# Wider spreads of the key roots, angle steps placed around the first product, and the convolution given out one quad sooner

## The chip, the cores and the metric

The kernel runs on one core of one Trainium2 chip. The metric is the device time of one execution in microseconds (us), the median of several runs. The engines are TensorE (PE, matrix products), VectorE (DVE), ScalarE (ACT), GpSimd (POOL) and SyncE (SP, which only issues DMAs here).

## The reference

One layer of a gated parallel decoder block, for 2048 tokens of width 1024, all in float32:

```python
h = rms_norm(x, norm_w) * (1 + scale) + shift            # shift, scale, gate from silu(c) @ w_ada + b_ada
a, b, g_conv, q, k, v, g_attn, m_conv, m_attn = split(h @ w_in)
u = depthwise_causal_conv(a * sigmoid(b), conv_w, conv_b)     # 31 taps
y_conv = (silu(layer_norm(u)) * silu(g_conv)) @ w_conv_out
q, k = rope(rms_norm(q)), rope(rms_norm(k))              # per head of 128
o = softmax-weighted sum over three groups of dilated causal windows, 4 heads each
y_attn = (o * silu(g_attn)) @ w_attn_out
out = x + gate * ((sigmoid(m_conv) * y_conv + sigmoid(m_attn) * y_attn) @ w_out)
```

Windows and dilations of the groups are (128, 1), (512, 4) and (2048, 16). The angle of rope is the token's position times a frequency; its cosine and sine are tables of 64 frequencies by 2048 tokens. The root of the mean square of a head enters q and k as a factor for each token.

## The kernel before

**Products.** A float32 product is made of three products of split operands: each operand is a high part (an activation on ScalarE) and the rest (a subtraction on DVE or POOL). The projection h @ w_in is worked in two halves of 1024 tokens. Within a half it goes by *quads*: two columns of 128 channels by two blocks of 512 tokens, made with seven products in place of eight (Strassen's scheme, `PRODUCTS` in line 164), from the quarters A11, A12, A22 and sums S1 to S4 of h. The first job of half 0 is plain instead, with sixteen products (`PLAIN`, line 299) for the v columns of two pairs of heads. One product is twelve matmul instructions (lines 305 to 309) and is called a *slot*; the order of slots is written out in advance (lines 1006 to 1029), and PE works through it in program order.

**The agenda.** Everything else is hung on slots. `at_slot(s, f, where)` (line 465) enters a piece of work, and the loop over slots (lines 1442 to 1483) runs, in this order: what is entered as `enter`, `load`, `act`, `pe`, `vec`; the split of the weights three slots ahead (`prepare`); `act2`; the slot's own product with its eviction; `tail`; `store`; the splits of landed quarters; and `run_conv`. Every engine is a queue in this written order (`manual_schedule`), so an instruction that waits holds up all that stands behind it on its engine. `tail` work of PE comes behind the twelve instructions of its slot.

**The start** (lines 1120 to 1191). h is made from x by a root of the mean square of each token and by scale and shift. ScalarE squares (`x_square`), PE sums (`x_sum`), DVE copies the rows of sums (`x_rows`), PE turns them and POOL takes the root (`x_roots`), PE spreads the roots over partitions (`x_spread`), DVE multiplies (`x_scale`); PE makes scale and shift from `w_ada` (`ada_mm`), and `ada_mod` adds the bias; `first_part` makes the high and the low part of a quarter. `angles()` yields the nineteen steps of the tables, DVE work but for the two sines of step 17; nine are issued before the sums, eight behind the roots, two behind the scaling. `tables_turn` (POOL) orders the tables for the dilated groups and `tables_keep` stores them (SP); they are read again at slot 19. The second block of tokens and the second part of the modulation follow in the slots 0 to 7 (`start_0` to `start_5`).

**Queries and keys** (`rotate`, lines 574 to 692). For a quad of two heads, ScalarE squares, PE sums over the head's channels into one bank (`sums`), ScalarE evicts the sums (`rows`), PE turns them (`turned`), DVE adds the epsilon (`more`), POOL raises to the power -1/2 (`roots`). For a query that is all; the root is applied later. For a key, PE spreads the roots over the channels by products with the identity (`spread`, line 629), one call for each half of the tokens, both into a bank of the tag "t", of which there is one; DVE multiplies (`key_scale`, line 635). The names are `rsk` (the bank), `stk` (mean squares and roots), `pssk` and `pssq` (sums).

**Gates and convolution.** The rest of a half are 22 quads: eight `ab_quad` make a * sigmoid(b), the other fourteen make gates. `gate_jobs` (line 995) orders them: `FIRST_GATES` gates, then each ab quad followed by `BETWEEN` gates. An ab quad that ends enters the 50 operations of its convolution (`conv_parts`, nearly all on DVE), and `run_conv` gives out 3.1 of them a slot (`CONV_RATE`). What is left is given out at once in slot 4 of the second half (`rope_again`). The attention of the half's last heads runs beside the first gates. In the last two quads of half 0 the quarters of the second half are loaded (line 1469), and two slots later they are split.

## Time and profile before

| | us |
|---|---|
| median of 3 runs (lowest, highest) | 2428.83 (2426.19, 2432.19) |
| profiled execution, its own time | 2426.46 |
| its span, from the first to the last instruction | 2424.7 |
| PE busy | 2321.6 (96%) |
| DVE, ACT, POOL busy | 1764.5, 1071.8, 1090.0 |

A row of the timeline gives the start, the duration, the engine, the line, the operation, what it writes and reads, its shape, how many instructions were merged, and in brackets the idle time of the engine before it with what ended it. A row of groups gives count, busy time, mean length in ns and idle time before. The granted clock is 1.00 when PE had its full clock. Names carry no buffer numbers: `paq`, `pak`, `pav` are banks of query, key and value quads, `spare_hi` and `spare_lo` the scratch in which a quad's result stands, `ce`, `cq`, `us`, `ca` the tiles of the convolution.

### The profile page before, as it was taken

The page shows a single profiled execution, that of the slowest core. Times are in us where ns is not written, and L with a number is a line of the kernel's source. Part 1 is how long each engine was busy: PE and PEld are TensorE (multiplying, and loading weights), DVE is VectorE, ACT ScalarE, POOL GpSimd, SP SyncE. Part 2 cuts the span into 40 slices and gives each one's busy share as a digit, 9 for nine tenths or more (in the row PEclk, how much of TensorE's full clock was granted, in tenths as well). Part 3 has the DMA queues.
Part 4 walks back from the last instruction along what each step waited for, and adds up shares of the span by engine and source line. Part 5 has one row for each costly group of instructions (what it writes and reads, how often), then busy time and mean ns, then how long its engine had stood idle before and what let it go on. Part 6 is the DMA issues. An engine that isn't in the chain of part 4 may idle for free.

```text
span 2424.7 us, 35722 instructions
## 1 busy us (share of the span) xinstructions
PE 2321.6 (96%) x12054; PEld 1884.0 (78%) x12054; DVE 1764.5 (73%) x2926; ACT 1071.8 (44%) x2159; POOL 1090.0 (45%) x844
## 2 busy tenths in 40 slices
PE   5998899999999999989999999999999999999999
PEld 3776678878778888767788887887888877888887
DVE  6877685553899999936666447469999988787644
ACT  3664445445554444634445444653444444332221
POOL 3455554445446688835433433445566640000221
PEclk8999999999999999989999999999999999999999
DMA  8366666567544446643565665856445469865553
GB/s 300 116 190 208 212 192 191 177 201 240 181 159 159 152 161 202 197 148 105 172 181 176 192 183 155 266 165 190 142 131 155 140 212 331 302 236 187 178 157 109
DMA packets 304111, 451.61 MB, mean 186 GB/s; under 512 B 29236, under 2 KB 132788, under 8 KB 303928
## 3 DMA queue, kind: packets, MB, share of 16 engines
q1 hardware_dynamic: 289656, 423.62, 55.1%
q10 hardware_dynamic: 14272, 25.72, 2.9%
q8 instruction: 95, 1.56, 0.3%
q14 instruction: 88, 0.72, 0.1%
HBM read 284.98 MB, written 164.24 MB: 185 GB/s over the span
## 4 chain that ended last, share of the span: by engine, by line
PE 72%; DVE 9%; DMA 3%; issue 2%; POOL 1%; ACT 1%; SPq 0%; DVEq 0%; ACTq 0%; POOLq 0%
PE yc L1518 7%; PE paab L309 6%; PE oa L1800 4%; PE pak L309 3%; PE paq L309 3%; PE pag_ma_d L309 3%; PE pcab L309 3%; PE pav L309 3%; PE pag_mc_d L309 3%; PE po L809 3%; PE ya L1518 3%; PE ps L756 3%; PE pag_g_d L309 2%; PE pck L309 2%; PE pcq L309 2%
## 5 line engine op out<-in xcount | busy, mean ns | idle before, releaser
L247 POOL TENSOR_TENSOR slT<-wT,shT 128x512 fp32r<-128x512 f32 x188 | 254.1, 1352 | 314.0 <-ACT shT L246 266.7
L247 POOL TENSOR_TENSOR slB<-wB,shB 128x512 fp32r<-128x512 f32 x142 | 193.4, 1362 | 151.7 <-ACT shB L246 144.4
L246 ACT ACTIVATE shB<-wB 128x512 fp32r<-128x512 f32 x234 | 147.2, 629 | 197.2 <-issue 40.5
L247 POOL TENSOR_TENSOR slT<-wB,shT 128x512 fp32r<-128x512 f32 x98 | 131.0, 1341 | 192.0 <-ACT shT L246 171.2
L246 ACT ACTIVATE shT<-wT 128x512 fp32r<-128x512 f32 x192 | 120.2, 627 | 149.4 <-issue 22.5
L367 DVE SCALAR_TENSOR_TENSOR ce<-ut,chan,ce 128x512 f32<-128x512 f32 x240 | 180.3, 751 | 3.7
L396 DVE SCALAR_TENSOR_TENSOR ce<-us,pair_taps,ce 128x512 f32<-128x512 f32 x240 | 180.7, 753 | 3.1
L768 DVE CUSTOM_DVE_ANT_0 sm<-ps,mask,rqq 128x256 f32<-128x256 f32 (+1 forms) x192 | 78.1, 444 | 120.5 <-PE ps L756 93.3
L380 DVE SCALAR_TENSOR_TENSOR cq<-ut,chan,cq 128x512 f32<-128x512 f32 x208 | 156.2, 751 | 0.0
L241 POOL TENSOR_TENSOR wB<-wB,wB 128x512 f32<-128x512 f32 x80 | 112.5, 1407 | 47.8 <-DVE slB L247 35.8
L246 ACT ACTIVATE shT<-wB 128x512 fp32r<-128x512 f32 x120 | 75.3, 627 | 78.5 <-PE paab L309 25.7
L786 DVE COPY pT<-ptp 128x512 f32<-128x512 f32 (+2 forms) x96 | 58.9, 614 | 55.0 <-PE ptp L784 54.9
L137 POOL TENSOR_SCALAR stf<-stf 128x4 f32<-128x4 f32 x4 | 2.1, 516 | 188.2 <-DVE stf L1556 141.8
L247 DVE TENSOR_TENSOR slB<-wB,shB 128x512 fp32r<-128x512 f32 x92 | 71.4, 776 | 16.8 <-ACT shB L246 14.6
L809 PE MATMUL po<-v,pT 128*128 128x128 f32 x560 | 81.9, 277 | 0.0
L1728 ACT ACTIVATE yh<-yq 128x512 fp32r<-128x512 f32 x48 | 27.3, 623 | 120.6 <-POOL yq L1722 46.4
L809 PEld LDWEIGHTS po<-v,pT 128*128 128x128 f32 x560 | 74.9, 191 | 6.1 <-issue 1.5
L756 PE MATMUL ps<-qk 128*128 128x128 f32 x512 | 75.6, 275 | 0.0
L756 PEld LDWEIGHTS ps<-qk 128*128 128x128 f32 x512 | 66.2, 192 | 0.3 <-issue 0.2
L775 ACT ACTIVATE sm<-sm,osb 128x256 f32<-128x256 f32 (+1 forms) x128 | 58.4, 459 | 8.7 <-DVE osb L768 3.3
L617 POOL TENSOR_TENSOR stk<-stk,mhalf 128x16 f32<-128x16 f32 x12 | 38.4, 3203 | 49.6 <-DVE stk L613 37.9
L815 ACT ACTIVATE osb<-po 128x256 f32<-128x256 f32 x64 | 24.7, 385 | 74.7 <-PE po L809 73.8
(808 smaller groups left out, 7758.2 us busy)
## 6 DMA issues: line engine op xcount, KB each, us to landing
wB<-in_w_in_dram SPq DMA_DIRECT2D x274, 256.0 KB, 4.3
wT<-tT_d SPq DMA_DIRECT2D x152, 256.0 KB, 3.0
tT_d<-wB SPq DMA_DIRECT2D x114, 256.0 KB, 3.5
qk<-qk_d SPq DMA_DIRECT2D x96, 256.0 KB, 4.3
v_d<-vev SPq DMA_DIRECT2D x48, 256.0 KB, 3.3
qk_d<-spare_hi SPq DMA_DIRECT2D x48, 256.0 KB, 3.8
qk_d<-spare_lo SPq DMA_DIRECT2D x48, 256.0 KB, 3.7
v<-v_d SPq DMA_DIRECT2D x96, 128.0 KB, 4.0
```

The costliest lines, as they stand in the source:

```text
L241: nc.gpsimd.tensor_tensor(dst, x0, x1, op=ALU.subtract)
L246: nc.scalar.activation(h, q[name], AF.Copy)
L247: eng.tensor_tensor(l, q[name], h.bitcast(F32), op=ALU.subtract)
L309: nc.tensor.matmul(ps, x, y, start=(first and m == 0), stop=(last and m == 11), skip_group_check=True)
L367: stt(box["e"], e[:, 1 + j : 513 + j], chan[:, cb, 2 * j : 2 * j + 1], box["e"], op0=ALU.mult, op1=ALU.add)
L380: stt(box["o"], o[:, 2 + j : 514 + j], w, psum_o, op0=ALU.mult, op1=ALU.add)
L396: stt(dst, box["both"][:, 1 + j : 513 + j], pair_taps[:, cb, j : j + 1], box["e"], op0=ALU.mult, op1=ALU.subtract if j == 0 else ALU.add)
L756: nc.tensor.matmul(ps[:, c : c + P], box["q"][i], kt, start=True, stop=True)
L768: nc.vector.tensor_tensor_reduce(sm[:, a:z], ps[:, a:z], m[:, 256 - (z - a) :], rq[:, b, u % 2 : u % 2 + 1], 3e38, ALU.add, ALU.min, box[" ...
L809: nc.tensor.matmul(po[:, P * i : P * i + P], box["pT"][:, c : c + P], vt, start=(m == 0), stop=(m == count[i] - 1))
L1518: nc.tensor.matmul(pz, w, xx, start=(m == 0), stop=(m == len(terms) - 1))
L1800: nc.tensor.matmul(ps, y, w, start=(m == 0 and ps.name not in begun), stop=(m == 11 and not more), skip_group_check=True)
```

## The change

- The epsilon is added by ScalarE as the sums are evicted (`rows`, now with a bias), `turned` moves from behind the product of its slot into its middle (a new place `mid`, after six of the twelve instructions), and `more`, now a copy, moves from DVE in the next slot to ScalarE behind the same slot's product.
- For a key, ScalarE widens the roots to 64 columns each (`widen`, two activations of 512 columns), and one `spread` makes eight full products of 128 columns in place of sixteen of 64, in the slot in which the first half was spread before, with a bank for each half ("t" and "u"). `key_scale` stays where it was. The first sums of squares come one slot later, since they use "u" as well.
- In the start, five angle steps stand before the sums, two behind the roots, three behind the scaling, and nine in the slots 1 to 3. The turns of the tables move from POOL to ScalarE, in the slots 4 to 6, and into landing buffers; their stores move to the slots 4 to 7. The second part of the modulation is made one slot sooner, the row of it is evicted before slot 4's product, A12 is made behind slot 4, and the last four scalings move behind slot 5.
- In half 0 two gates stand before the first ab quad in place of three, and three behind the last in place of two.
- The landing buffers of the quarters are six in place of four, and their splits come three slots after the load in place of two.

```diff
@@ -38,7 +38,7 @@
 GROUPS = (1, 2, 0)
 WS, WR, AHEAD = 4, 10, 3
 QKV_LO = (((1, 3, 5), (1, 3, 5), (0, 1, 3, 5, 6)), ((), (), (1, 3, 5)))
-FIRST_GATES, BETWEEN = 3, ((1, 1, 1, 1, 2, 1, 2, 2), (1, 1, 2, 1, 1, 1, 1, 3))
+FIRST_GATES, BETWEEN = (2, 3), ((1, 1, 1, 1, 2, 1, 2, 3), (1, 1, 2, 1, 1, 1, 1, 3))
 CONV_RATE = 3.1
 MANUAL, ORDER_END = (True, True), 6
 LATER_X, LATER_ROOM, LATER_BUSY = 21, 2, 1
@@ -139,6 +139,8 @@
 
     edge = ctx.enter_context(pool("edge", side="right"))
     edge_tile = edge.tile([P, 56], F32, name="edge")
+    eps = edge_tile[:, 55:56]
+    nc.gpsimd.memset(eps, EPS)
     hpool_c = [tc.tile_pool(name=f"hT{i}", bufs=1, side="right", reuse_waits="tile") for i in range(2)]
     hpools = [c.__enter__() for c in hpool_c]
 
@@ -307,6 +309,8 @@
         terms = [t for k in range(4) for t in ((wh[:, k], ah[:, k]), (wh[:, k], al[:, k]), (wl[:, k], ah[:, k]))]
         for m, (x, y) in enumerate(terms):
             nc.tensor.matmul(ps, x, y, start=(first and m == 0), stop=(last and m == 11), skip_group_check=True)
+            if m == 5:
+                run_agenda(slot_now[0], "mid")
 
     def quad(name, got, sink):
 
@@ -600,7 +604,7 @@
 
         def rows():
             r = box["rows"] = rb["p"].tile([P, 2, P], F32, tag="rows", name=f"ssr{n}", bufs=1)
-            nc.scalar.activation(r.rearrange("p c i -> p (c i)"), box["pr"][:, : 2 * P], AF.Copy)
+            nc.scalar.activation(r.rearrange("p c i -> p (c i)"), box["pr"][:, : 2 * P], AF.Identity, bias=eps)
 
         def turned():
             pt = box["pt"] = bank("t", f"prq{n}")
@@ -610,7 +614,7 @@
         def more():
             st = box["st"] = rb["p"].tile([P, 32], F32, tag="st", name=f"st{n}", bufs=2)
             got = box["pt"][:, : 2 * P].rearrange("p (c q m) -> p c q m", c=2, q=4)[..., :2]
-            nc.vector.tensor_scalar(st[:, :16].rearrange("p (c q m) -> p c q m", c=2, q=4), got, EPS, None, op0=ALU.add)
+            nc.scalar.activation(st[:, :16].rearrange("p (c q m) -> p c q m", c=2, q=4), got, AF.Copy)
 
         def roots():
             st = box["st"]
@@ -620,19 +624,22 @@
                 nc.gpsimd.tensor_scalar(rq, st[:, 16:32], ISQ, None, op0=ALU.mult)
                 heads_rq[half, u0] = rq.rearrange("p (b m) -> p b m", m=2)
 
-        def spread(c):
-            def f():
-                rs = box["rs"] = bank("t", f"rs{n}_{c}")
+        def widen():
+            box["wide"] = rp["p"].tile([P, 16, 64], F32, tag="wide", name=f"rw{n}", bufs=1)
+            for c in range(2):
+                sl = slice(8 * c, 8 * c + 8)
+                nc.scalar.activation(box["wide"][:, sl], box["st"][:, 16 + 8 * c : 24 + 8 * c][:, :, None].to_broadcast([P, 8, 64]), AF.Copy)
+
+        def spread():
+            box["rs"] = [bank("tu"[c], f"rs{n}_{c}") for c in range(2)]
+            for c in range(2):
                 for q in range(4):
-                    for m in range(2):
-                        a = 16 + 8 * c + 2 * q + m
-                        nc.tensor.matmul(rs[64 * m : 64 * m + 64, P * q : P * q + P], box["st"][:, a : a + 1].to_broadcast([P, 64]), ident,
-                                         start=True, stop=True, skip_group_check=True)
-            return f
+                    w = box["wide"][:, 8 * c + 2 * q : 8 * c + 2 * q + 2].rearrange("p m r -> p (m r)")
+                    nc.tensor.matmul(box["rs"][c][:, P * q : P * q + P], w, ident, start=True, stop=True)
 
         def key_scale(c, i):
             x = reg[i][:, 512 * c : 512 * c + 512]
-            return lambda: tt(x, x, box["rs"], op=ALU.mult)
+            return lambda: tt(x, x, box["rs"][c], op=ALU.mult)
 
         def store(i):
             def f():
@@ -667,7 +674,7 @@
             count = (2,) * 6
         for s, c, i in sq:
             at_slot(s, square(c, i), "act" if s > e6 else "act2")
-            at_slot(max(s, e6 - 2), sums(c, i), "tail")
+            at_slot(max(s, e6 - 1), sums(c, i), "tail")
         ops = rope()
         assert sum(count) == 12
         for d, k in enumerate(count):
@@ -676,15 +683,16 @@
                 at_slot(start + d, lambda: next(ops)())
         end = start + len(count)
         at_slot(last, rows, "act")
-        at_slot(last, turned, "tail")
-        at_slot(last + 1, more)
+        at_slot(last, turned, "mid")
+        at_slot(last, more, "tail")
         at_slot(last + 1, roots)
         if which == 0:
             for i in range(2):
                 at_slot(end, store(i), "load")
         else:
+            at_slot(last + 2, widen, "act2")
+            at_slot(last + 2, spread, "tail")
             for c in range(2):
-                at_slot(last + 2 + c, spread(c), "tail")
                 for i in range(2):
                     at_slot(last + 3 + c, key_scale(c, i))
             assert last + 3 + 1 >= end - 1
@@ -908,9 +916,12 @@
             nc.tensor.matmul(acc[32 * q : 32 * q + 32, :256], wide[:, k], landed_ada(g, k)[:, q // 2, 256 * (q % 2) : 256 * (q % 2) + 256],
                              start=(k == 0), stop=(k == KC - 1))
 
-    def ada_mod(g, acc, tag):
+    def ada_row(g, acc):
         row = su.tile([P, 512], F32, tag="sq", name=f"row{g}", bufs=5)[:, :256]
         nc.scalar.activation(row, acc[:, :256], AF.Copy)
+        return row
+
+    def ada_mod(g, row, tag):
         pa = bank(tag, f"pt_ada{g}")
         for i in range(2):
             nc.tensor.transpose(pa[:, P * i : P * i + P], row[:, P * i : P * i + P], ident)
@@ -958,17 +969,19 @@
         yield lambda: v.tensor_tensor(a, a, a, op=ALU.mult)
         yield lambda: v.tensor_scalar(a, a, -2.0, 1.0, op0=ALU.mult, op1=ALU.add)
 
-    def tables_turn(g):
-        for src, dst in ((ang, permuted), (sng, nag)):
-            if g == 1:
-                nc.gpsimd.tensor_copy(dst.rearrange("p (t r i) -> p t r i", t=2, r=4), src.rearrange("p (t i r) -> p t r i", t=2, r=4))
-            else:
-                nc.gpsimd.tensor_copy(dst.rearrange("p (r t i) -> p r t i", t=2, r=16), src.rearrange("p (t i r) -> p r t i", t=2, r=16))
-
-    def tables_keep(g):
-        for i, src in enumerate((permuted, nag) if g else (ang, sng)):
-            for half in range(2):
-                nc.sync.dma_start(tab_d[half, g, i], src[64 * half : 64 * half + 64])
+    def table(g, i):
+        return landing[4 - 2 * g + i][:, :1024] if g else (ang, sng)[i]
+
+    def table_turn(g, i):
+        src, dst = table(0, i), table(g, i)
+        if g == 1:
+            nc.scalar.activation(dst.rearrange("p (t r i) -> p t r i", t=2, r=4), src.rearrange("p (t i r) -> p t r i", t=2, r=4), AF.Copy)
+        else:
+            nc.scalar.activation(dst.rearrange("p (r t i) -> p r t i", t=2, r=16), src.rearrange("p (t i r) -> p r t i", t=2, r=16), AF.Copy)
+
+    def table_keep(g, i):
+        for half in range(2):
+            nc.sync.dma_start(tab_d[half, g, i], table(g, i)[64 * half : 64 * half + 64])
 
     turning = angles()
 
@@ -995,7 +1008,7 @@
     def gate_jobs(half):
         todo = [(gate_quad, half, g, cb) for g in ((MC0, mc_d, AF.Tanh), (MA0, ma_d, AF.Tanh), (GC0, g_d, AF.Silu)) for cb in range(0, KC, 2)]
         todo[9:9] = [(ag_quad, half, None, cb) for cb in (0, 2)]
-        got = [todo.pop(0) for _ in range(FIRST_GATES)]
+        got = [todo.pop(0) for _ in range(FIRST_GATES[half])]
         for cb in range(KC):
             got.append((ab_quad, half, None, cb))
             for _ in range(BETWEEN[half][cb]):
@@ -1117,13 +1130,13 @@
         for j in range(2):
             weight(j, name)
 
-    angle_steps(9)
+    angle_steps(5)
     pm = bank("t", "xm0")
     for k in range(KC):
         x_square(k, 0)
         x_sum(k, 0, pm)
     st = x_roots(0, pm, x_rows(0, pm))
-    angle_steps(8)
+    angle_steps(2)
     pr = x_spread(0, st, bank("u", "xr0"))
     acc = bank("o", "ada0")
     for k in range(KC):
@@ -1132,12 +1145,11 @@
     prepare(1)
     for k in range(KC):
         x_scale(k, 0, pr)
-    angle_steps(2)
-    ada_mod(0, acc, "t")
+    angle_steps(3)
+    ada_mod(0, ada_row(0, acc), "t")
     for k in range(4):
         first_part("A11", k, 0)
     prepare(2)
-    tables_turn(1)
 
     box = {}
 
@@ -1171,24 +1183,31 @@
             ada_mm(1, box["acc"], k)
 
     def start_5():
-        ada_mod(1, box["acc"], "t")
+        ada_mod(1, box["row"], "t")
+
+    def start_6():
         for k in range(4, KC):
             first_part("A12", k, 0)
-        for k in range(4, KC):
-            x_scale(k, 1, box["pr"])
 
     at_slot(0, start_0, "tail")
     at_slot(1, start_1, "pe")
     at_slot(1, start_2, "tail")
     at_slot(2, start_3, "tail")
-    at_slot(4, start_4, "tail")
-    at_slot(5, start_5, "tail")
+    at_slot(3, start_4, "tail")
+    at_slot(4, start_5, "tail")
+    at_slot(4, start_6, "tail")
     for k in range(4, KC):
+        at_slot(5, lambda k=k: x_scale(k, 1, box["pr"]), "tail")
         at_slot(6 + (k - 4) // 2, lambda k=k: first_part("A22", k, 1), "tail")
-    at_slot(1, lambda: tables_keep(0), "store")
-    at_slot(1, lambda: tables_keep(1), "store")
-    at_slot(2, lambda: tables_turn(2), "store")
-    at_slot(4, lambda: tables_keep(2), "store")
+    at_slot(4, lambda: box.update(row=ada_row(1, box["acc"])), "act2")
+    at_slot(1, lambda: angle_steps(3))
+    at_slot(2, lambda: angle_steps(4))
+    at_slot(3, lambda: angle_steps(2))
+    for i, (g, s, to) in enumerate(((1, 4, 5), (2, 5, 6), (1, 6, 7), (2, 6, 7))):
+        at_slot(s, lambda g=g, i=i: table_turn(g, i // 2), "act2")
+        at_slot(to, lambda g=g, i=i: table_keep(g, i // 2), "store")
+    for i in range(2):
+        at_slot(4, lambda i=i: table_keep(0, i), "store")
 
     tt = lambda dst, x0, x1, op: nc.vector.tensor_tensor(dst, x0, x1, op=op)
     stt = lambda dst, x0, by, x1, op0, op1: nc.vector.scalar_tensor_tensor(dst, x0, by, x1, op0=op0, op1=op1)
@@ -1466,9 +1485,9 @@
         if i == half_jobs - 1:
             asked += [(PRODUCTS[n][0], k) for k in range(4)]
         for name, k in asked[:2]:
-            raw = gpa["p"].tile([P, 512], F32, tag="ai" if k == 3 else "gt", name=f"landing{name}_{k}", bufs=2 if k == 3 else 4)
+            raw = gpa["p"].tile([P, 512], F32, tag="ai" if k == 3 else "gt", name=f"landing{name}_{k}", bufs=2 if k == 3 else 6)
             nc.sync.dma_start(raw, quarter_src(name, k))
-            held.append((s + 2, lambda name=name, k=k, raw=raw: quarter_split(1, name, k, raw, nc.gpsimd if k == 3 else nc.vector)))
+            held.append((s + 3, lambda name=name, k=k, raw=raw: quarter_split(1, name, k, raw, nc.gpsimd if k == 3 else nc.vector)))
         del asked[:2]
         due += CONV_RATE
         if not conv_todo:
```

## The prediction

> **What bounds the kernel now.** I read the page first, then the busy time by stage, then the waits of TensorE (PE), then the timeline at each of its longer stops.
>
> ```profile
> span 2424.7 us, 35722 instructions
> PE 2321.6 (96%) x12054; PEld 1884.0 (78%) x12054; DVE 1764.5 (73%) x2926; ACT 1071.8 (44%) x2159; POOL 1090.0 (45%) x844
> ```
>
> PE is busy for 96% of the span, so a microsecond is won only where PE stops, where its clock is halved, or where it has less to do. About 103 us of the span are stops. The stages show where (the columns are the stretch and its length, busy time of PE, PEld, DVE, ACT and POOL with their instructions, granted clock, DMA share, GB/s):
>
> ```profile
> 35.00:80.00 45.00, 37.62 (x228) 24.99 (x229) 23.65 (x32) 16.87 (x28) 17.71 (x11) 0.77 0.48 167
> 160.00:400.00 240.00, 218.76 (x1269) 170.96 (x1268) 170.30 (x242) 115.58 (x211) 122.08 (x79) 0.98 0.63 202
> 740.00:985.00 245.00, 245.00 (x1082) 202.89 (x1081) 235.89 (x343) 108.77 (x188) 195.25 (x156) 1.00 0.49 169
> 985.00:1070.00 85.00, 69.37 (x290) 55.45 (x289) 66.14 (x83) 40.53 (x68) 49.05 (x34) 0.90 0.50 160
> ...
> 600.00:620.00 20.00, 20.00 (x114) 17.18 (x113) 11.12 (x41) 12.20 (x37) 6.06 (x8) 1.00 0.51 162
> ...
> 700.00:720.00 20.00, 16.20 (x89) 13.30 (x88) 20.00 (x46) 9.46 (x26) 10.31 (x9) 1.00 0.48 158
> ```
>
> PE stands still for 7.4 us from 35 to 80 (with a mean clock of 0.77), 21.2 us in the key and query quads from 160 to 400, and 15.6 us at the change of halves (985 to 1070). With the wait for the first product, at 35, these are the places that the change touches. From 740 to 985 PE never stops (245 / 1082 = 0.23 us a product, so 2.7 us for a slot of twelve), but DVE is at 96% there: the convolution has it nearly full. The list of PE's waits gives who ended them, their sum, number and longest:
>
> ```profile
> PE rsk L629 <- POOL stk L617: 13.1, 6, 4.2
> ...
> PE rsk L629 <- DVE spare_lo L635: 6.4, 4, 2.1
> ...
> PE pssk L597 <- ACT sqk L584: 4.1, 2, 2.5
> ...
> PE rsk L629 <- DVE spare_hi L635: 3.1, 2, 1.7
> ```
>
> **The change part by part: the start.** Rows of the timeline before (start, duration, engine, line):
>
> ```profile
> 10.57 3.44 PE L880 MATMUL xm<-xsq,ones 128*32 128x128 f32 x40 [0.45 <-ACT xsq L875]
> ...
> 16.32 1.23 DVE L955 SCALAR_TENSOR_TENSOR spare_hi<-spare_hi 128x1024 f32<-128x1024 f32 x1
> 17.46 0.28 DVE L885 COPY xrow<-xm 128x128 f32<-128x128 f32 x1
> ...
> 20.62 2.08 PE L897 MATMUL xr<-ident,xst 128*128 128x128 f32 x8 [2.28 <-POOL xst L892]
> ...
> 26.61 4.86 DVE L902 TENSOR_TENSOR hf<-hf,xr 128x512 f32<-128x512 f32 x8
> ...
> 34.95 0.80 PE L309 MATMUL pC<-A_hi,shB_p 128*128 128x512 f32 x1 [4.28 <-ACT A_hi L937]
> 35.51 0.69 DVE L939 TENSOR_TENSOR A_lo<-hf,A_hi 128x512 fp32r<-128x512 f32 x1
> 36.12 0.55 DVE L938 TENSOR_SCALAR hf<-hf,mod 128x512 f32<-128x512 f32 x1
> ...
> 38.93 4.69 POOL L964 COPY spare_lo<-spare_hi 128x1024 f32<-128x1024 f32 x2
> 41.80 2.37 DVE L939 TENSOR_TENSOR A_lo<-hf,A_hi 128x512 fp32r<-128x512 f32 x1
> ...
> 44.23 0.80 PE L309 MATMUL pC<-A_lo,shB_p 128*128 128x512 f32 x1 [2.97 <-DVE A_lo L939]
> ...
> 45.38 1.51 PE L880 MATMUL xm<-xsq,ones 128*32 128x128 f32 x24
> ...
> 48.69 0.52 PE L309 MATMUL pC<-A_lo,shB_p 128*128 128x512 f32 x1
> ```
>
> The sums of squares end at 14.0 (10.57 + 3.44), but the copy of their rows comes behind nine angle steps and starts at 17.46. With five steps ahead of it it can start at once, 3.4 us sooner, and the spread, 5.2 us later on this row (20.62 + 2.08 - 17.46), ends at about 19.3. Then the eight scalings (4.86) run from 19.3 to 24.2 instead of behind the angles at 26.61; three angle steps (1.23 each) end at 27.9; the modulation and the first part took 34.95 - 33.7 = 1.3 us from DVE's work on the modulation. First product at about 29.3: **-5.6 us**. In the first slot the twelve products took 45.38 - 34.95 = 10.4 us, because the fourth low part waited: 2.37 us for a subtraction that takes 0.69, beside POOL's table copies of 4.69. Those copies go to ScalarE slots later, so a part costs 0.55 + 0.69 and four parts set a slot of about 6.4 us (1.3 + 3 x 1.24 + three products at half speed, since the clock before was not granted in full from 34.95 to 48.69): **-4 us**. The full clock came 4.5 us after the last stop, at 44.23; what is left at half speed in the second slot is worth **-1 us**.
>
> By the Trainium skill ("TensorE: Matmul & The Clock Gate", What's actually happening) one busy window of some 3.4 us opens the clock. By it the second half of the new first slot would already run at full speed, and the sum would be 1 us better. The rows above agree only so far: products with stops between them did not open it in 13.7 us.
>
> ```profile
> 71.24 0.51 PE L309 MATMUL pC<-A_hi,shB_p 128*128 128x512 f32 x1 [1.30 <-ACT A_hi L937]
> ...
> 72.55 0.57 PE L309 MATMUL pC<-A_lo,shB_p 128*128 128x512 f32 x1 [0.81 <-DVE A_lo L939]
> ...
> 78.60 0.63 PE L309 MATMUL pC<-A_lo,shB_p 128*128 128x512 f32 x1
> 79.03 0.63 PE L309 MATMUL pC<-A_hi,slB_p 128*128 128x512 f32 x1
> ```
>
> The second modulation comes one slot sooner, so A12 has a whole slot (some 2.8 us) to be made. The stops of 1.30 and 0.81 us go, and with them the half clock from 72.55 to 79.03 (15 products 0.43 apart against 0.23: 3.2 us). DVE still needs 1.24 us for a part that PE uses in 0.7, so I leave 1 us of wait: **-4.3 us**. What moves into these slots: nine angle steps on DVE in the slots 1 to 3 (at most 9 x 1.23 = 11 us; PE's own work there, three slots of 2.7 with the sums, spread and modulation products between them, is some 15), the sines on ScalarE in slot 2 ahead of A21, four table turns on ScalarE in the slots 4 to 6 ahead of the splits of weights, and the twelve table stores on SP, whose readers come at slot 19. A turn of 1024 columns takes twice what 512 take below, 1.3 to 2.2 us; behind it on ScalarE stand the splits for three slots later, and past that cover PE would wait, so 0 to 4 us lost. Start in all: -14.9, less 1 for this, **-14** (-7 to -18).
>
> **The roots of the keys.** The page's row of a contiguous activation of 512 columns, then one key quad of the timeline, then the two kinds of spread (each product shows as two instructions):
>
> ```profile
> L246 ACT ACTIVATE shB<-wB 128x512 fp32r<-128x512 f32 x234 | 147.2, 629 | 197.2 <-issue 40.5
> ...
> 209.60 1.11 ACT L505 ACTIVATE spare_hi<-paq 128x512 f32<-128x512 f32 x1 [2.02 <-PE paq L309]
> ...
> 216.08 3.31 POOL L617 TENSOR_TENSOR stk<-stk,mhalf 128x16 f32<-128x16 f32 x1 [2.64 <-DVE stk L613]
> ...
> 219.44 0.98 PE L629 MATMUL rsk<-ident,stk 128*64 128x128 f32 x7 [4.15 <-POOL stk L617]
> ```
>
> ```profile
> 55.49 1.05 PE L897 MATMUL xr<-ident,xst 128*128 128x128 f32 x8
> ...
> 56.30 0.48 PE L309 MATMUL pC<-A_hi,shB_p 128*128 128x512 f32 x1
> ...
> 1179.80 1.09 PE L629 MATMUL rsk<-ident,stk 128*64 128x128 f32 x16
> 1180.82 0.66 PE L784 MATMUL ptp<-ident,sm 128*128 128x128 f32 x4
> ```
>
> The mean squares waited on DVE until 216; POOL, free at 213.4, stood 2.64 us for them, and PE then 4.15 for POOL. Moved to ScalarE the copy follows the eviction (209.60 + 1.11) and is done by 210.9, so POOL raises to the power from 213.4 to 216.8, widening (512 columns: 0.63 like the contiguous row, at most the 1.11 of the strided eviction) adds 0.6 before the first half can be spread, and PE waits for about 2 instead of 4.15. So the 13.1 us fall to POOL's own backlog; I take half, **-6.5**. The 9.5 us (6.4 + 3.1) are the second half waiting for the one bank that DVE still read; it has its own bank now: **-9.5**. The first sums of squares come a slot later: of the 4.1 us of waits on ScalarE's squares I take **-3**. Halved clock after the two stops of 4 us is worth **-3** (240 us at 0.98 are 4.8).
>
> PE's own work: the sixteen instructions of eight half-wide products took 1.02 us until the next began (1179.80 to 1180.82), the eight of four full ones 0.81 (55.49 to 56.30). Half-wide pairs already run two at a time, so halving their number saves little; 0.2 for each of 24 spreads, **-5** (0 to -7).
>
> The Trainium skill ("TensorEngine Tiling (Array Packing)", Theoretical Speedup) gives products of at most 64 columns up to twofold speed, as two tiles work side by side. By it four full products take as long as eight half-wide ones, and the sum would be 5 us smaller; the rows agree but for 0.21 us.
>
> Added: 24 widenings of 0.6 us on ScalarE and 24 copies of 16 values (the rows with the bias added are the activation of before). ScalarE is a queue in order: behind a widening that waits for the power stand the eviction of the next product and the splits. No row shows it; the bounds are 0 and the present 13.1, and as ScalarE is at 48% I take 0.4 a quad, **+5**. PE also meets DVE sooner (adds, key scales; the stage has DVE at 71%): **+5** of its gain given back. Transposing the rows inside the product costs nothing while the eviction of the rows precedes it, else up to 1 us a quad. Sum -6.5 - 9.5 - 3 - 3 - 5 + 5 + 5: **-17** (0 to -28).
>
> **Convolution one quad sooner.**
>
> ```profile
> 1015.18 0.80 PE L309 MATMUL pav<-A_hi,shB 128*128 128x512 f32 x1 [5.48 <-ACT spare_hi L446]
> ...
> 1029.94 7.88 DVE L396 SCALAR_TENSOR_TENSOR ce<-us,pair_taps,ce 128x512 f32<-128x512 f32 x10
> ...
> 1042.34 0.77 PE L309 MATMUL pcv<-S_hi,shT 128*128 128x512 f32 x1 [9.06 <-DVE spare_hi L507]
> ```
>
> A block of channels is 50 DVE operations, 3.1 of them are given out in a slot. The last block becomes ready 14 slots before the half ends, so 43 fit and the rest stands ahead of the adds of the second half. Now it has 21 slots: twelve fewer operations in the last 14 slots and none behind them, some 20 of 0.79 us (7.88 / 10), 16 us. That is as much as PE's stops of 15.6, and the half clock that follows them (85 us at 0.90, about half of it with PE at work) is worth 4. I take **-17** of these 19.6. The work goes to the quad before, where DVE has room (11.1 of 20 us from 600 to 620) but attention still runs: once both overlap DVE is full and PE loses up to 3.8 us in 20 (700 to 720). One quad more of it is **+2** (0 to 6). The landing buffers and their splits a slot later hide behind it, since a part is used some twelve slots later, in the next half.
>
> **Sum**: -14 - 17 - 17 + 2 = -46 us against the profiled execution, 2426.46 (a span of 2424.7 and 1.8 around it), so 2380.5. The median of the runs, 2428.83, lies 2.4 above: **2383 us**.
>
> **Rivals.**
> 1. The hole at the change of halves stays: DVE, at 96% from 740 on, only moves its backlog, and PE pays in the attention instead. For it: PE already stops there. Against it: 9 idle us of DVE from 600 to 620. Then -17 + 2 becomes -3: 2395.
> 2. The roots gain nothing: POOL's backlog and ScalarE's blocked queue eat the 17 us: 2400. For it: POOL starts at 213.4 whatever DVE does.
> 3. The start goes better and POOL falls in step (-18, -28, -19, 0): 2429 - 65 = 2364.
> 4. Slower: ScalarE stands at each widening behind POOL's power; the eviction of the next product stands behind it, and PE stops for the bank, with its clock halved afterwards. The other parts bring 14 + 17 - 2 = 29 us, so it decides from 29 / 12 = 2.4 us lost in each of the twelve key quads; with the present longest stop, 4.15, in each it is 50 - 29 = 21 slower: 2450. Against it: the longest stop at a spread now is 4.2, the mean of the six 2.2, and ScalarE is half idle.
>
> **How the numbers follow.** The forecast has 0.6, the rivals 0.14, 0.12, 0.10 and 0.04. The range from 2362 to 2405 holds the first four and leaves out little beyond. A change under 0.3% (7 us) can't be told from none: faster 0.94, same 0.02, slower 0.04.
>
> **What would show it.** The first product near 29 us, no half clock near 73; spread waits under 8 us in all, none on key scales; no PE stop over 3 us between 985 and 1070; slightly more stops on attention's minima from 600 on. It is wrong if ScalarE's widening becomes PE's releaser, if convolution still runs past the half, or if splits behind the table turns stop PE before 90 us.

## The result, and the profile after

The changed kernel takes 2396.46 us (median of 4 runs, 2391.25 to 2400.4) beside 2430.51 of before (4 runs): a ratio of 0.9855, 95% interval 0.9821 to 0.9889. Timed again later beside other runs it took 2394.76 us against 2428.96, 0.9869 (0.9856 to 0.9883). So it is 1.3 to 1.5% faster, 32 to 35 us where 46 were forecast; the time lies in the range forecast, 12 to 14 us above its likeliest value. The execution whose profile follows took 2400.4, the longest of its four.

The page's head, then the same stretches as before (columns as in the prediction: stretch, length, busy PE, PEld, DVE, ACT, POOL, clock, DMA share, GB/s):

```profile
span 2398.6 us, 35365 instructions
...
PE 2319.5 (97%) x11862; PEld 1892.1 (79%) x11862; DVE 1751.2 (73%) x2902; ACT 1093.7 (46%) x2211; POOL 1083.1 (45%) x841
```

```profile
35.00:80.00 45.00, 39.81 (x255) 28.36 (x255) 34.09 (x44) 27.76 (x34) 9.87 (x7) 0.87 0.52 170
160.00:400.00 240.00, 219.37 (x1201) 175.05 (x1201) 167.61 (x237) 117.40 (x221) 119.68 (x78) 0.96 0.61 196
985.00:1070.00 85.00, 79.42 (x354) 65.16 (x353) 48.84 (x58) 46.75 (x78) 52.44 (x36) 0.96 0.59 191
```

The start and the change of halves (985 on) have fewer stops and a better clock. The key and query quads of the first half (160 to 400) are as full of stops as before, and at a lower clock (0.96 against 0.98). The list of PE's waits shows what took the place of the old ones (sum, number, longest):

```profile
PE rsk L638 <- ACT rwk L631: 12.3, 4, 4.9
...
PE pav L311 <- ACT spare_hi L450: 5.6, 1, 5.6
PE pta L838 <- DVE osb L820: 5.5, 3, 3.8
...
PE prqk L612 <- ACT ssrk L607: 4.3, 2, 2.4
```

The 9.5 us on the key scales are gone. The 13.1 us behind POOL's power are now 12.3 behind ScalarE's widening (13.8 in a second execution), and the transposition in the midst of a product brought 4.3 of its own.

Where the time went is seen best by the start of the same product before and after. The table gives, for a profiled execution of each kernel, how much shorter (-) or longer (+) each stretch became: the start of the product that ended the stretch in the new trace less its start before (155.2, 529.8, 965.5, 1085.4 and 1513.0 us), less the same difference at the stretch before; the last column takes the rest from the spans. The second of these products is the first of a gate: the last key quad of the half ends just ahead of it, with its second spread at 524.49 in the profile before. The experiments of the next section stand beside it.

```profile
524.49 1.09 PE L629 MATMUL rsk<-ident,stk 128*64 128x128 f32 x16 [1.74 <-DVE spare_hi L635]
```

| kernel | ratio of times (95%) | start | keys, half 0 | attention, gates | change of halves | keys, half 1 | rest |
|---|---|---|---|---|---|---|---|
| changed | 0.9855 (0.9821-0.9889) | -7.5 | -2.4 | +4.8 | -11.7 | -10.4 | +1.2 |
| changed, timed again | 0.9869 (0.9856-0.9883) | -8.5 | -5.2 | +4.8 | -12.8 | -10.3 | +1.4 |
| start alone | 0.9966 (0.9953-0.9979) | -10.6 | +0.2 | +0.3 | +1.2 | +2.0 | +0.1 |
| roots alone | 0.9932 (0.9920-0.9944) | -1.3 | -4.3 | 0.0 | +1.3 | -10.0 | +1.4 |
| convolution alone | 0.9974 (0.9963-0.9986) | +0.7 | -0.1 | +4.8 | -12.4 | +1.4 | +1.9 |
| turns a slot later | 0.9866 (0.9847-0.9885) | -5.2 | -10.3 | +4.9 | -14.2 | -10.2 | +1.9 |
| no turns | 0.9856 (0.9836-0.9876) | -10.7 | -7.3 | +5.5 | -7.6 | -9.8 | +0.4 |
| widening first | 0.9830 (0.9810-0.9849) | -9.8 | -8.9 | +4.4 | -12.8 | -11.4 | -0.3 |
| half-wide, two banks | 0.9819 (0.9801-0.9837) | -8.5 | -12.5 | +2.7 | -13.1 | -10.4 | +1.9 |
| half-wide, one bank | 0.9900 (0.9886-0.9913) | -11.3 | -6.5 | +4.1 | -11.9 | -0.7 | +2.4 |
| rows behind | 0.9844 (0.9827-0.9860) | -9.2 | -8.6 | +6.8 | -14.3 | -10.4 | +0.7 |
| one gate | 0.9841 (0.9824-0.9859) | -10.6 | -6.8 | +6.1 | -16.8 | -10.5 | +0.7 |
| half-wide, one gate | 0.9820 (0.9807-0.9834) | -6.2 | -16.1 | +5.5 | -18.3 | -10.5 | +3.2 |

Kernels with the same start differ by up to 5 us in that column (-6.2 to -11.3), so a single execution tells a stretch only to some 3 us either way; a verdict below that rests on a smaller difference is called open.

### The profile page after: what moved, and what is told of

Read it like the earlier page. It is cut to its first block, busy times and chain, and to the rows that moved or that the text cites. A ratio compares the mean times of both kernels' runs of the same rounds, so it can differ in the third digit from the quotient of the medians.

```text
span 2398.6 us, 35365 instructions
## 1 busy us (share of the span) xinstructions
PE 2319.5 (97%) x11862; PEld 1892.1 (79%) x11862; DVE 1751.2 (73%) x2902; ACT 1093.7 (46%) x2211; POOL 1083.1 (45%) x841
## 4 chain that ended last, share of the span: by engine, by line
PE 74%; DVE 7%; DMA 3%; ACT 1%; issue 1%; SPq 1%; POOL 0%; ACTq 0%; DVEq 0%; POOLq 0%
PE yc L1537 7%; PE paab L311 6%; PE pak L311 4%; PE pav L311 4%; PE oa L1819 4%; PE paq L311 4%; PE pag_ma_d L311 4%; PE pcab L311 3%; PE po L817 3%; PE ya L1537 3%; PE ps L764 3%; PE pag_mc_d L311 2%; PE pag_g_d L311 2%; PE pck L311 2%; PE pcv L311 2%; PE oc L1819 2%
## 5 line engine op out<-in xcount | busy, mean ns | idle before, releaser
L243 POOL TENSOR_TENSOR wT<-wB,wB 128x512 f32<-128x512 f32 x40 | 56.8, 1420 | 2.0
L243 POOL TENSOR_TENSOR wB<-wB,wT 128x512 f32<-128x512 f32 x40 | 56.8, 1420 | 0.0
```

What stands on the lines that cost most here:

```text
L243: nc.gpsimd.tensor_tensor(dst, x0, x1, op=ALU.subtract)
```

## The experiments

**The three parts, each alone.** Each takes the hunks of one part of the change and leaves the others as before (for instance, the convolution alone):

```diff
-FIRST_GATES, BETWEEN = 3, ((1, 1, 1, 1, 2, 1, 2, 2), (1, 1, 2, 1, 1, 1, 1, 3))
+FIRST_GATES, BETWEEN = (2, 3), ((1, 1, 1, 1, 2, 1, 2, 3), (1, 1, 2, 1, 1, 1, 1, 3))
```

> The kernel before with the edits of the start alone. Theory (the places are separate and add up): the first product near 31 us, the plain job ends some 7 us sooner as in the changed kernel, and nothing later moves: 7 us faster. Rival (the start's gain is taken back in the first key quads, where POOL is behind): under 3 us faster, with longer stops at the spreads of half 0. The step of the prediction says 14 us.

> The kernel before with the edits of the queries' and keys' roots alone. Theory: some 3 us won in half 0, where POOL and ScalarE are late, and some 10 us in half 1, where DVE's hold on the one bank goes: 13 us faster. Rival (the widening is what PE now waits for everywhere): no more than 5 us. The step of the prediction says 17 us.

> The kernel before with the gate order of half 0 and the landing buffers alone. Theory: the stop of 9 us at the second value quad of half 1 goes with its half clock (12 us), the stop of 5.5 us before it stays, and attention beside convolution costs some 5 us more: 7 us faster. Rival (both stops depend on the whole backlog of DVE): both go and 15 us are won. The step of the prediction says 15 us.

Measured against 2428.38 (15 runs): 2420.43, 2412.88 and 2423.4 us, so -8.0, -15.5 and -5.0, together -28.5. That is near the theories, which were written after the result was known (7, 13 and 7), and under the steps of the prediction (14, 17 and 15). The whole brought 32 to 35 in other calls; with some 3 us of uncertainty in each part the difference isn't explained further. The convolution alone shows both of its sides, PE's rows in attention and at the change of halves:

```profile
692.53 0.69 PE L830 MATMUL pta<-ident,osb 128*128 128x128 f32 x2 [3.76 <-DVE osb L812]
...
1020.15 0.79 PE L309 MATMUL pav<-A_hi,shB 128*128 128x512 f32 x1 [5.51 <-ACT spare_hi L446]
```

The stop of 9.06 us is gone, the one of 5.48 stays as 5.51, and attention now waits for DVE.

**The start: what holds A12.** In the changed kernel PE stops again where the second modulation begins. The rows of the timeline:

```profile
57.07 1.67 DVE L970 TENSOR_SCALAR spare_hi<-spare_hi 128x1024 f32<-128x1024 f32 x1
58.66 0.15 DVE L930 TENSOR_TENSOR mod<-pt_ada,cols 128x8 f32<-128x8 f32 x1
58.77 2.02 ACT L978 ACTIVATE ada_hi<-spare_hi 128x1024 f32<-128x1024 f32 x1 [3.45 <-DVE spare_hi L970]
60.70 2.92 ACT L948 ACTIVATE A_hi<-hf,mod 128x512 fp32r<-128x512 f32 x4
61.55 0.49 PE L311 MATMUL pC<-A_hi,shB_p 128*128 128x512 f32 x1 [1.31 <-ACT A_hi L948]
62.86 0.50 PE L311 MATMUL pC<-A_lo,shB_p 128*128 128x512 f32 x1 [0.82 <-DVE A_lo L950]
...
68.52 0.80 PE L311 MATMUL pC<-A_lo,shB_p 128*128 128x512 f32 x1 [0.67 <-DVE A_lo L950]
```

ScalarE stands for DVE's last angle step, turns a table for 2.02 us, and only then makes A12's first high part. The first trial moves the turns a slot later:

```diff
-    for i, (g, s, to) in enumerate(((1, 4, 5), (2, 5, 6), (1, 6, 7), (2, 6, 7))):
+    for i, (g, s, to) in enumerate(((1, 5, 6), (2, 6, 7), (1, 7, 8), (2, 7, 8))):
```

> The changed kernel with the four turns of the tables each one slot later (slots 5, 6, 7, 7 in place of 4, 5, 6, 6), so that no turn stands ahead of A12 on ScalarE. Theory (ScalarE stood at the first turn for DVE's last angle step, and A12 behind it): the stops near 61.5 us (1.3, 0.8, 0.5, 0.7 us) shrink under 1 us in all and the clock stays full after them: 4 to 6 us faster than the changed kernel, 38 to 40 faster than before. Rival (DVE itself makes A12 too late): the stops stay over 2 us and the time of the changed kernel.

It took 2395.55 us, no different from the changed kernel. The stops around 61 shrink to 2.3 us in all (the longest 0.72 and 1.18), but two new ones come behind DVE's splits of weights. DVE is full there (busy for all of the 12 us from 99 on), with operations that take 1.74 us where the shortest of their line takes 0.68:

```profile
100.52 0.50 PE L311 MATMUL pbq<-A_hi,slB 128*128 128x512 f32 x1 [0.65 <-DVE slB L249]
...
108.38 1.74 DVE L1212 TENSOR_TENSOR hf<-hf,hf 128x512 f32<-128x512 f32 x1
110.04 0.68 DVE L249 TENSOR_TENSOR slT<-wB,shT 128x512 fp32r<-128x512 f32 x1
...
110.78 0.50 PE L311 MATMUL pcq<-S_hi,slT 128*128 128x512 f32 x1 [3.57 <-DVE slT L249]
```

The second trial leaves the turns out:

```diff
     def table(g, i):
-        return landing[4 - 2 * g + i][:, :1024] if g else (ang, sng)[i]
+        return (ang, sng)[i]
     def table_turn(g, i):
-        src, dst = table(0, i), table(g, i)
...
+        return
```

> The changed kernel without the four table turns on ScalarE: the tables are stored unturned, so the rotation of the heads that need the other order works with wrong angles; all other work is done. Theory (ScalarE stood 3.45 us for DVE's last angle step before the first turn, and a turn of 2.0 us stands ahead of A12's first part): the stops of 1.31, 0.82, 0.50 and 0.67 us between 61 and 69 go with their half clock, and the first key spread begins 3 to 5 us sooner than 158.2; in all 3 to 6 us faster than the changed kernel. Rival A (DVE itself is late for A12, by the angle steps): the stops stay, nothing gained. Rival B (the stop is only moved, as when the turns went a slot later: PE stops near 100 to 110 on DVE's share of the weight splits): the stops near 61 go, one of 2 to 4 us comes near 110, nothing gained.

It took 2392.51 us; the intervals of it and of the changed kernel overlap. Its rows around A12:

```profile
56.65 1.67 DVE L970 TENSOR_SCALAR spare_hi<-spare_hi 128x1024 f32<-128x1024 f32 x1
58.24 0.15 DVE L930 TENSOR_TENSOR mod<-pt_ada,cols 128x8 f32<-128x8 f32 x1
...
58.63 2.94 ACT L948 ACTIVATE A_hi<-hf,mod 128x512 fp32r<-128x512 f32 x4 [3.72 <-DVE mod L932]
...
60.81 0.50 PE L311 MATMUL pC<-A_lo,shB_p 128*128 128x512 f32 x1 [0.74 <-DVE A_lo L950]
64.14 0.50 PE L311 MATMUL pC<-A_lo,shB_p 128*128 128x512 f32 x1 [1.17 <-DVE A_lo L950]
66.28 0.79 PE L311 MATMUL pC<-A_lo,shB_p 128*128 128x512 f32 x1 [1.18 <-DVE A_lo L950]
```

The stop for the high part (1.31) is gone, those for the low parts are as long as before or longer. ScalarE still stands 3.72 us, now for the modulation itself: on DVE it is queued behind the last two angle steps, which end at 58.3. The first key spread begins at 155.1, no sooner than with the turns in the execution called "one gate" (155.2). So the turn was one cause and not the main one; DVE is late for A12, by the steps that were moved into slot 3 and then by its own 1.24 us a part. (That these two steps are what delays the modulation is read from the rows; no kernel was run without them.)

How much the stops cost depends on the clock behind them. From 60 to 85 the changed kernel and the one called "one gate", which are the same up to there, had:

```profile
60.00:85.00 25.00, 21.61 (x74) 15.73 (x73) 19.49 (x26) 17.42 (x19) 4.17 (x3) 0.80 0.56 167
```

```profile
60.00:85.00 25.00, 23.24 (x97) 18.03 (x98) 21.63 (x29) 20.63 (x26) 6.04 (x4) 0.93 0.53 162
```

Both stop for 1.3 and 0.8 us at the first two products of A12. In the first the half clock begins two products later and lasts from 63.5 to 73.8, through the later stops; in the second it begins at once and is over by 65.0, and the later stops are then shorter (0.42 and 0.22). The column "start" follows it in eight executions of this start: those with 10 us of half clock behind A12 have -7.5 to -8.5 (three), those with 6.8 us -9.2 and -9.8, those with 3.4 us -10.6 to -11.3 (three). The -6.2 is not explained by it (3.4 us there too).

**The roots: the widening.** Two key quads of the changed kernel show what PE waits for (POOL, ScalarE and PE around 210, then around 270):

```profile
206.89 3.38 POOL L621 TENSOR_TENSOR stk<-stk,mhalf 128x16 f32<-128x16 f32 x1
210.30 1.15 ACT L631 ACTIVATE rwk<-stk 128x512 f32<-128x512 f32 x2 [5.57 <-POOL stk L621]
210.98 3.78 PE L638 MATMUL rsk<-ident,rwk 128*128 128x128 f32 x16 [4.02 <-ACT rwk L631]
...
263.49 3.39 POOL L621 TENSOR_TENSOR stk<-stk,mhalf 128x16 f32<-128x16 f32 x1 [2.10 <-ACT stk L617]
269.51 0.81 ACT L1283 ACTIVATE xl<-xl,mod 128x512 f32<-128x512 f32 x1 [1.88 <-DVE xl L1282]
270.75 1.13 ACT L631 ACTIVATE rwk<-stk 128x512 f32<-128x512 f32 x2
271.42 3.50 PE L638 MATMUL rsk<-ident,rwk 128*128 128x128 f32 x16 [4.90 <-ACT rwk L631]
```

Near 210 POOL is late (it begins without a pause behind other work) and ScalarE stands 5.57 us for it. Near 270 POOL is done at 266.9, but ScalarE first waits for DVE with a scaling that stands ahead of the widening, and widens only at 270.75. Two trials take this apart. One puts the widening first in its slot, the other takes it out and spreads half-wide into the two banks:

```diff
-            at_slot(last + 2, widen, "act2")
+            at_slot(last + 2, widen, "act")
```

```diff
-                    w = box["wide"][:, 8 * c + 2 * q : 8 * c + 2 * q + 2].rearrange("p m r -> p (m r)")
-                    nc.tensor.matmul(box["rs"][c][:, P * q : P * q + P], w, ident, start=True, stop=True)
+                    for m in range(2):
+                        a = 16 + 8 * c + 2 * q + m
+                        nc.tensor.matmul(box["rs"][c][64 * m : 64 * m + 64, P * q : P * q + P], box["st"][:, a : a + 1].to_broadcast([P, 64]), ident,
+                                         start=True, stop=True, skip_group_check=True)
...
-            at_slot(last + 2, widen, "act2")
```

> The changed kernel with the widening put ahead of the slot's eviction and the other work on ScalarE in its slot. It tells what ScalarE's queue costs the widening, and what a widening that waits for POOL's power costs the rest of ScalarE. Theory (two of the six stops, at 271 and 1478, come from work ahead of the widening on ScalarE, some 2 to 4 us each; where POOL is late, near 210, ScalarE stands whichever place it has): spread stops fall from 12.3 to about 8 us and the eviction behind a waiting widening brings a new stop of 1 to 3 us: 2393 to 2399. Rival (ScalarE standing at the widening holds the evictions, as in the fourth rival of the prediction): a stop of 3 us or more on the bank of the next product in several quads, 2405 or more.

> The changed kernel with the widening on ScalarE taken out: each key quad again spreads its roots by sixteen half-wide products straight from POOL's result, but into two banks as the changed kernel has it. Theory (the gain of the roots is the second bank and the earlier start; the widening costs, the full products save as little as the rows of before said): the stops at a spread lose the widening's 0.6 us and the waits for ScalarE's queue, some 0.6 x 6 + 3 = 6 us of the 12.3, now put down to POOL, and PE's own work grows by 0.2 x 24 = 5 us: within 3 us of the changed kernel (2393 to 2399). Rival A (full products are worth twice the half-wide, some 0.4 us or more a spread): 10 us slower, 2406. Rival B (widening is what costs; half-wide pairs are as fast): 6 to 8 us faster, 2389.

Widening first took 2387.7 us, half-wide spreads 2386.46 (both beside 2428.42): 0.983 and 0.9819, where the changed kernel has 0.9869 with an interval (from 0.9856) above both of theirs (up to 0.9849 and 0.9837); its first and wider interval overlaps them. PE's waits at the spread fell to 8.4 us in the first, as its theory had it. In one row ScalarE stands 6.26 us for POOL, and no product waits behind that for an eviction, so the rival did not show; the one new wait, 2.1 us, is for DVE to read the bank "u" ahead of the next sums of squares. In the second the waits fell to 5.6:

```profile
PE rsk L638 <- ACT rwk L631: 8.4, 3, 3.4
```

```profile
209.09 1.15 ACT L631 ACTIVATE rwk<-stk 128x512 f32<-128x512 f32 x2 [6.26 <-POOL stk L621]
```

```profile
PE rsk L639 <- POOL stk L621: 5.6, 3, 2.7
```

What the products themselves cost is cleanest in the second half, where almost nothing waits. The busy time of the six spreads (second number) in the kernel before, the changed one and the half-wide one with two banks:

```profile
1085.00:1600.00 515.00, 13.12 (x192) 10.38 (x192) 15.33 (x24) 1.00 0.59 180
```

```profile
1085.00:1600.00 515.00, 11.89 (x96) 11.43 (x96) 15.26 (x24) 1.00 0.60 184
```

```profile
1085.00:1600.00 515.00, 11.80 (x192) 10.35 (x192) 15.26 (x24) 1.00 0.61 187
```

Eight full products cost PE 11.89 / 6 = 1.98 us a quad, sixteen half-wide ones 1.97: the same. By the time until the next instruction it is 1.78 and 1.90, in the same quad of the changed kernel and of the half-wide one:

```profile
1159.69 1.95 PE L638 MATMUL rsk<-ident,rwk 128*128 128x128 f32 x16
1161.47 0.60 PE L792 MATMUL ptp<-ident,sm 128*128 128x128 f32 x4
```

```profile
1145.80 1.97 PE L639 MATMUL rsk<-ident,stk 128*64 128x128 f32 x32
1147.70 0.66 PE L793 MATMUL ptp<-ident,sm 128*128 128x128 f32 x4
```

The 1.2 us less than before come with the half-wide products too; with one bank (next trial) the same figure is 13.42, so they belong to the second bank, which lets a quad's spread run in one piece. Theory and rival B each had a part: the stops shrank as the theory said (by 6.7 us), but the 5 us of PE that should have paid for them weren't there, and the variant is 8 to 12 us faster than the changed kernel.

**The roots: the second bank.** The same half-wide variant, but through the one bank, the second half of the columns a slot later:

```diff
-            at_slot(last + 2, spread, "tail")
             for c in range(2):
+                at_slot(last + 2 + c, spread(c), "tail")
```

> The variant with half-wide spreads straight from POOL's result, but through one bank as before: the second half of the columns is spread a slot later, when DVE has read the first. All else of the change stays (earlier sums, rows in the midst, the copy on ScalarE, the start, the convolution). Against the variant with two banks it tells what the second bank alone is worth. Theory (the stops on the key scales were real, 9.5 us and the half clock behind them, and nothing else covers them): they come back, 8 to 12 us slower than with two banks, 2394 to 2399. Rival A (the earlier start of the roots already moves the second half away from DVE's scaling): 3 us slower at most, 2389. Rival B (PE only meets the next late engine): no difference, 2386.

It took 2402.49 us beside 2428.96: 0.9900 against 0.9819, 16 us slower than with two banks (20 by the ratios), more than expected. The stops behind DVE are back, in the second half in nearly every key quad:

```profile
PE rsk L639 <- DVE spare_lo L645: 8.1, 5, 2.2
...
PE rsk L639 <- DVE spare_hi L645: 2.6, 2, 1.7
```

In the second half the second bank is worth 9.7 us (-0.7 against -10.4), all the gain there. Another 6.0 lie in the key quads of the first half (-6.5 against -12.5), in one execution only. There the changed kernel (-2.4 and -5.2) has the second bank and gains no more than the half-wide variant without it.

**The roots: the transposition in the midst.**

```diff
-        at_slot(last, turned, "mid")
+        at_slot(last, turned, "tail")
```

> The changed kernel with the key quads' rows transposed behind the slot's product again instead of in the midst of it. Theory (the two stops of 4.3 us at the transposition in the midst are the price of an earlier start of POOL, and POOL is late in half 0 through its own backlog): the 4.3 us go, the six spread stops get longer by about 1 us each where POOL was idle before them and not at all where it was behind: 2394 to 2400, no difference that can be told. Rival A (the move in the midst is what brought the gain of the roots): 8 us slower or more, 2405. Rival B (it brought nothing and costs its stops): 4 us and its half clock faster, 2390.

It took 2391.02 us, 0.9844; against the changed kernel, timed in other calls, 0 to 6 us faster, which is too little to call. The waits changed as the theory said: those at the transposition fall from 4.3 to 0.5, those at the spread grow from 12.3 to 14.5, the longest from 4.9 to 7.9 us. The move in the midst brought nothing that can be seen.

```profile
PE rsk L638 <- ACT rwk L631: 14.5, 4, 7.9
...
PE prqk L612 <- ACT ssrk L607: 0.5, 1, 0.5
```

**The convolution: yet one quad sooner.**

```diff
-FIRST_GATES, BETWEEN = (2, 3), ((1, 1, 1, 1, 2, 1, 2, 3), (1, 1, 2, 1, 1, 1, 1, 3))
+FIRST_GATES, BETWEEN = (1, 3), ((1, 1, 1, 1, 2, 1, 2, 4), (1, 1, 2, 1, 1, 1, 1, 3))
```

> The changed kernel with the convolution of the first half given out one more quad sooner (one gate ahead of attention instead of two, four quads after the last block instead of three). Theory (DVE is full from 740 to 1015, so work given out sooner only comes to stand beside attention): the stop of 5.6 us near 1010 shrinks by half or more, and PE loses 3 to 5 us more on attention's results between 600 and 740: 2393 to 2400, no difference that can be told. Rival (there is room left before 740): the stop goes and nothing is lost, 6 to 8 us faster with its half clock, 2389.

It took 2390.76 us, 0.9841: again 0 to 6 us from the changed kernel. The last stop of the change of halves falls from 5.6 to 1.9, and the stretch has its full clock:

```profile
PE pav L311 <- ACT spare_hi L450: 1.9, 2, 1.1
...
PE ptp L792 <- DVE stm L776: 3.2, 3, 1.2
```

```profile
985.00:1070.00 85.00, 81.97 (x398) 65.65 (x396) 38.76 (x36) 45.40 (x74) 52.13 (x36) 1.00 0.48 157
```

The stretch gains 4 to 5 us more than in the changed kernel (-16.8), and attention loses 1.3 more (+6.1), less than the theory had. So the stop was the convolution's; whether the trade pays is open by the times.

**The two best together.** The half-wide spreads with two banks and the one gate:

> Two variants together: half-wide spreads straight from POOL's result into two banks, and the first half's convolution one more quad sooner. Theory (the first saves ScalarE's widening in the key quads, the second moves a stop of 5 us from the change of halves to attention): 2382 to 2389, like the first alone. Rival (they add): 2380 or less.

2384.14 us beside 2428.96: 0.9820 (0.9807 to 0.9834), the same as the half-wide variant alone, as the theory had it, and faster than the changed kernel timed with it (2394.76; their intervals don't meet). The change of halves gained 5.2 us more than with the half-wide spreads alone, attention gave 2.8 of it back; the rest is within the spread of the start. The changed kernel again, timed as a yardstick:

> The changed kernel as it is, timed beside the three that follow, because its own interval was too wide to tell it from the variants. Both theories: 2390 to 2397. If it comes out at 2391 or less, then taking the widening out and putting it first brought 3 to 4 us at most; at 2395 or more they brought 7 to 9.

At 2394.76 it is next to the second of the two cases: putting the widening first brought 7 us, taking it out 8.

## Why the prediction was right, and where it wasn't

**The start, -14: half of it.** The first product came 4.0 us sooner (4.8 in the second execution) for the 5.6 forecast, at 30.98. Two of the three angle steps behind the scaling took 2.17 us and not 1.23, beside POOL's split of weights. The first slot then gained 3.6 us for 4, the second 1.0 for 1. The step that failed is "The stops of 1.30 and 0.81 us go": they stand in the profile after as 1.31 and 0.82, with 0.50 and 0.67 behind them and the half clock for 10 us. Of that term, -4.3, nothing came: the start of the third product was 8.6 us sooner than before, that of the tenth only 7.3. I had given A12 a whole slot from the sooner modulation, and counted the nine angle steps only by their sum; two of them stand on DVE ahead of the modulation, and the first turn ahead of the high part on ScalarE. The Trainium skill ("TensorE: Matmul & The Clock Gate", What's actually happening) opens the clock after one busy window of some 3.4 us and has that window run free of the kernel. The rows agree in kind: behind the same two first stops the half clock lasted 10 us in one execution and 3.4 in another, and every stretch of half clock in the start of these traces lasted 3.4 us or a multiple of it (6.8, 10, 13.7 or 17).

**The roots, -17: 13 to 15 in the whole kernel by the stretches, 15.5 alone by the times.** The term for two banks, -9.5, is what the second half alone shows (9.7 with and without); with the first half the bank is worth some 16, so the term was too small. "The 13.1 us fall to POOL's own backlog; I take half" failed for the kernel as changed and holds without the widening (5.6 us): POOL is earlier, as forecast, and the widening hands the gain to ScalarE's queue. ScalarE's +5 was too small: taking the widening out brought 8 to 12 us. With the loss at the spreads, the transposition's stops and the half clock the first half's key quads gained 2.4 and 5.2 us (6.8 in "one gate", which is the same up to there) where the half-wide variants with two banks gained 12.5 and 16.1. "0.2 for each of 24 spreads, -5" was mis-sized. It set four full products in the start (0.81 us to the next instruction) against eight half-wide ones in a key quad (1.02). In the key quads themselves, where nothing stops and the clock is full, eight full products take 1.70 to 1.89 us to the next instruction, and sixteen half-wide ones 1.90 in one piece and 2 x 1.02 in two: some 0.1 us a quad for the full products and 0.14 for the one piece, together 3 us in twelve quads. Here the rule of the Trainium skill that the prediction set beside it ("TensorEngine Tiling (Array Packing)", Theoretical Speedup: products of at most 64 columns up to twice as fast, two tiles side by side) agrees with the trace: 11.80 us for 96 half-wide products, 11.89 for 48 full ones.

**The convolution, -17 + 2: 7 to 8 in the whole kernel by the stretches, 5.0 alone by the times.** The stop of 9.06 us and its half clock went, -11.7 and -12.8 at the change of halves. "That is as much as PE's stops of 15.6" failed for the other stop, which stayed at 5.6: DVE remains full there (busy for 29.7 of the 30 us from 985 on) with the convolution and the splits of landed quarters, which the sum of 16 us had not counted. In the row below, the splits of the changed kernel take up to 1.8 us each on DVE, where 0.68 is the least:

```profile
L184 DVE TENSOR_TENSOR S_lo<-landingS,S_hi x12: 679/960/1787, 989.0 to 1020.3; 128x512 fp32r<-128x512 f32 x12
```

The price in attention was +4.8, with the convolution alone and in the whole kernel, inside the bounds of 0 to 6 but not at 2; the roots alone change nothing there.

**The rivals.** The fourth's mechanism is there (ScalarE stands 5.57 and 6.26 us at a widening), but no eviction behind it stopped PE, even with the widening first: no slower case. The second, that POOL and ScalarE eat the gain of the roots, holds for most of the first half's gain and not for the second half. The first describes the convolution in part: one of two stops stayed. That the time came out next to the first rival's 2395 is chance: there the start and the roots bring all of their 31 us. The profiled executions, which lie 4 and 1 us above their medians, fall 20 and 16 us short of the 46: some 6 are the start, 2 to 4 the roots, 7 to 8 the convolution, and 1 comes behind the last stretch.

**The signs.** The time lies in the range, but by the signs that the prediction named much of its mechanism failed. Its sign of no wait on a key scale came true, and the first product, at 30.98, came near the 29 named. The half clock near 73, spread waits under 8 us (12.3) and no stop over 3 us at the change of halves (5.6) did not. Two of the three signs of being wrong appeared: ScalarE's widening is PE's releaser, and the convolution still runs past the half. Its last operation stands on DVE at 1015.71, where the second half's first product begins at 1010.4 (in the kernel before at 1042.7 and 1015.18). So the total lies in the range although the gain of each of the three parts was put too high.

## What to carry to other kernels

A stop that is taken from one engine's queue and given to another's is gained only if nothing stands ahead of it in the new queue: look up what the engine does in that slot, by name, before pricing a moved operation at its own length. When several edits stand together, look for the one that carries the gain (here a second bank, with some 16 us) and try the change without the rest: without the widening and the full products it was 8 to 12 us faster. Steps moved "into room" on an engine must be placed against each waiting row there, not against the engine's idle time.

## What was not expected of the hardware

Behind the same two stops the half clock lasted 10 us in one execution and 3.4 in another, which goes with 2 to 4 us in the start of the whole. Vector operations on 1024 columns took 2.17 us beside a POOL subtraction and 1.23 alone. In the kernel without turns one subtraction of 512 columns on DVE, whose like takes 0.68, took 8.83, while POOL ran operations without a gap; PE then stopped 4.88 us for a copy behind it. It was seen once, and its cause stays open.

```profile
968.31 8.83 DVE L184 TENSOR_TENSOR A_lo<-landingA,A_hi 128x512 fp32r<-128x512 f32 x1
```
